# A trunk kernel's odd input stage: two pairs of column blocks in seven products, the third in plain chunks, and the mixing weights fetched in the gate stage

## The chip, the cores and the metric

One core of a Trainium2 chip runs the kernel. The metric is device time in microseconds (us). The kernel before took 1264.31 us, the median of 3 runs (1264.02 to 1265.02).

## The reference, cut to what matters

Two layers work on a sequence of 256 rows and 2048 features in fp32. Layer 0 (even) is a recurrence and an attention; layer 1 (odd) is a gated unit with position mixing. After each layer a gate stage adds a projected per-layer input. The change touches the odd layer and the gate stage ahead of it:

```python
def odd_mixer(hn, w_in, ln_g, ln_b, w_s, b_s, w_out):
    u, v, g = jnp.split(hn @ w_in, 3, axis=-1)        # three times 2048 columns
    u = jax.nn.gelu(u)
    v = layer_norm(jax.nn.gelu(v), ln_g, ln_b)
    ...                                               # v in chunks of 128 positions, 16 groups of 128
    mixed = jnp.einsum('gts,bcsgd->bctgd', ws, vc) + b_s.T[:, :, None]
    y = u * mixed.reshape(bsz, t, SG_WIDTH) * jax.nn.silu(g)
    return y @ w_out

h = h + per_layer_embedding(h, p[layer], pe_w[layer], pe_gate_norm[layer], pe_w_gate[layer])
```

## The kernel before, in words

Every large product multiplies 256 rows by a 2048 x 512 block of a weight matrix. Rows and weights are each split into a high and a low fp32r part, and a product is the sum of three matmuls (high by high, high by low, low by high). Weights stream through the core in chunks of 128 x 1024 fp32 (512 KB): two k-tiles of 128 rows by 512 columns.

`program` (L955) writes the list `self.chunks` for the whole kernel and then walks it. For each chunk, `feed` (L159) keeps loads (`issue_load`, L140, on SyncE's queue) up to nine chunks ahead and splits (`issue_split`, L146) three chunks ahead: ScalarE copies the raw chunk to `hi` (L152), VectorE subtracts to get `lo` (L153). Then the chunk's matmuls are issued, and unless the chunk is marked `half`, `advance` (L119) moves every task on by one step. A task is a generator with the work on a finished block: scaling, gelu, transposing, storing. `until` (L130) makes a task wait for another's result. Tiles of 128 x 512 fp32 come from one pool of 52 buffers (`buf`, L87), PSUM has 8 banks (L88), raw chunks have 14 buffers (L85), split chunks 5 (L86).

Two kinds of work fill the list. A **plain** block (`unit`, L168, by `wunit`, L195) is eight chunks of twelve matmuls of 512 columns (lines L186 to L188, tile `pg`): two row tiles, two k-tiles, three products. A **pair** (`spair`, L203) computes two column blocks at once, 1024 columns, by a scheme of seven products in place of eight on the half-size parts of the row and weight matrices: 28 chunks of six matmuls (lines L226 to L228, into the banks `Z`, `V`, `U`). Three of the seven weight operands come straight from memory; the other four are made in place: once a chunk has been split, GpSimd issues a DMA that adds the next weight chunk to the raw tile (L157), and that sum is split later as the next chunk of the chain. The row operands are differences that `sums` (L288) makes from the transposed rows; they are split like the rows (`ssum`). What the banks hold is put together by small adds (L234 to L259) into SBUF tiles.

The odd input stage has 12 column blocks, four each for v, u and g. In the kernel before, blocks 0 and 1 of each of the three are a pair and blocks 2 and 3 are plain (L983 to L985): 84 pair chunks and 48 plain ones. `zip` (L273) lists them so that one plain chunk follows every two pair chunks, and so that the first product of the next pair stands before the last product of this one. The tasks are `ov_task` (L853: scale, gelu, statistics), `ou_task` (L906: scale, gelu), and `og_task` (L929: silu, product, transpose, split for the next stage), which waits for `mix_task` (L912), which waits for the normalised v and for u. When all four v blocks are there, `ln` (L867) normalises them in the order 2, 3, 0, 1: for each block it fetches gain and bias rows, spread over 128 partitions, on SyncE's queue (L885), then VectorE does two passes per row tile (L889, L890):

```python
        for c in (2, 3, 0, 1):
            g = self.t(name="lng")
            b = self.t(name="lnb")
            for x, src in ((g, "ln_g"), (b, "ln_b")):
                ap = self.a[src]
                nc.sync.dma_start(x, bass.AP(tensor=ap.tensor, offset=ap.offset + c * 512, ap=[[0, 128], [1, 512]]))
```

`odd_params` (L894), started with the third plain block, fetches the mixing weights on GpSimd's queue in four tiles and clears a corner of each after it has landed (L902). The stage behind is the odd output projection (`add_h_task` with layer 1), whose chunks are taken in the order 4, 5, 6, 7, 2, 3, 0, 1. Ahead of the odd stage stands the gate stage of layer 0 (`gate_layer`, L949; `gate_task`, L805): four blocks of one embedding chunk and eight plain ones. Each of its tasks stores the rows, transposes them and splits them for the odd stage (`to_acts`, L755).

Of the kernel before, what the change touches and what calls it, by code (L numbers as in the profile page):

```python
# [57 lines left out]

LOADS_AHEAD = 5
# [19 lines left out]
class Trunk:  # L79
# [121 lines left out]


    def spair(self, p, acts, sums, post):  # L203


# [13 lines left out]
        def mm(b, a, c):  # L219
            def f(hi, lo):  # L220
                new = first(b)
                for k in range(2):
                    j = 2 * c + k
                    wh, wl = hi[:, k * 512:(k + 1) * 512], lo[:, k * 512:(k + 1) * 512]
                    ah, al = a(j, 0), a(j, 1)
                    nc.tensor.matmul(st[b], ah, wh, start=new and k == 0, stop=False, skip_group_check=True)  # L226
                    nc.tensor.matmul(st[b], al, wh, start=False, stop=False, skip_group_check=True)  # L227
                    self.last_mm = nc.tensor.matmul(st[b], ah, wl, start=False, stop=(c == 3 and k == 1),  # L228
                                                    skip_group_check=True)
                if c == 3:  # L230
                    after[b].pop(0)()
            return f
# [31 lines left out]
        for b, w, chain, a in (("Z", 0, 0, x(0, 0)), ("V", 1, 0, z(1)), ("Z", 2, 1, x(1, 0)), ("U", 3, 0, z(2)),  # L264
                               ("V", 3, 2, z(3)), ("U", 1, 2, z(0)), ("U", 2, 0, x(1, 1))):
            for c in range(4):
                q = Chunk(blk(w, c), 1024, mm(b, a, c), half=c % 2 == 0)
# [20 lines left out]
    def sums(self, pt, g):  # L288

        nc = self.nc  # L290
        xe = self.t([128, T], name="xe")
        nc.scalar.activation(xe, pt[:, 0], AF.Copy, scale=g[:, 0:1])
        a11, a21 = xe[:, 0:128], xe[:, 128:256]
        a12, a22 = pt[:, 1, 0:128], pt[:, 1, 128:256]
        s = self.t([128, 4, 128], name="s")
        nc.vector.scalar_tensor_tensor(s[:, 1], a22, g[:, 1:2], a21, op0=OP.mult, op1=OP.subtract)
        nc.vector.tensor_tensor(s[:, 0], a11, a21, op=OP.subtract)
        nc.vector.scalar_tensor_tensor(s[:, 3], a12, g[:, 1:2], a11, op0=OP.mult, op1=OP.subtract)
# [450 lines left out]
    def squares(self, h, key, c, t):  # L749
        if c == 0 and t == 0:  # L750
            self.ss[key] = self.kept([128, 2, 4], "ss")
        j = self.t(name="junk")
        self.nc.scalar.activation(j, h, AF.Square, accum_out=self.ss[key][:, t, c:c + 1])

    def to_acts(self, hs, c, key, gain_col):  # L755

        for p in range(2):
# [5 lines left out]
            if key in self.summed:  # L763
                self.spawn(self.sums_task(key, j, self.sums(pt, g)))
        for t in range(2):
            self.squares(hs[t], key, c, t)
        if c == 3:
            self.rms(self.ss[key], key)
# [19 lines left out]

    def add_h_task(self, c, layer, ps):
        if layer == 1:  # L790
            self.h[c] = []
            for t in range(2):
                h = self.t(name="hr")
                nc = self.nc
                nc.sync.dma_start(h, self.hd[c, t])
                self.h[c].append(h)
# [4 lines left out]
        yield  # L801
        self.to_acts(hs, c, f"g{layer}", C_PG + 16 * layer)
        yield

    def gate_task(self, c, layer, ps):  # L805
# [3 lines left out]
        e = self.e.pop((layer, c))  # L809
        hs = self.h[c]  # L810
# [11 lines left out]
        if layer == 0:  # L822
            for t in range(2):
                self.hd[c, t] = self.dram.tile([128, 512], F32, name=self.name("hd"))
                nc.sync.dma_start(self.hd[c, t], hs[t])
            yield 2
            self.to_acts(hs, c, "o", C_NG + 16)
            del self.h[c]
# [37 lines left out]

    def ln(self):  # L867
# [26 lines left out]
    def odd_params(self):  # L894
        nc, a = self.nc, self.a
        self.bs = self.kept([128, 16], "bs")
# [32 lines left out]
    def og_task(self, c, ps):  # L929
# [10 lines left out]
        for p in range(2):  # L940
            o = p * T
            self.y[2 * c + p] = self.split(self.fm(ys[0][:, o:o + T], ys[1][:, o:o + T], "yt"), scale=0.25)
# [6 lines left out]
    def gate_layer(self, layer):  # L949
        for c in range(4):  # L950
            self.put(self.unit([self.a["pe_w"][layer, c]], lambda: self.pT[layer],
                               lambda ps, c=c: self.e.__setitem__((layer, c), ps), nk=2, bank=self.pa))
            self.put(self.wunit(lambda: self.hs[f"g{layer}"], self.post(self.gate_task, c, layer)))

    def program(self):  # L955
# [5 lines left out]
        self.st = None  # L961
        self.xs, self.ssum, self.summed, self.hd = {}, {}, {"o"}, {}
# [27 lines left out]
        self.put(plain[:4])  # L990
        self.zip(plain[4:], pairs)
        n = len(self.chunks)
        for c in range(4):
            wu(lambda: self.y, self.add_h_task, c, 1, order=[4, 5, 6, 7, 2, 3, 0, 1])
        self.chunks[n + 8].spawn.append(lambda: self.load_p(1))
        self.gate_layer(1)
# [71 lines left out]
def _layout(i):  # L1068
# [24 lines left out]
    parts += [tm(wo[2048:]), tm(wo[:2048]), tm(wg[0]), tm(ov[:, 1024:]), tm(ou[:, 1024:]), tm(og[:, 1024:]), tm(oo), tm(wg[1])]  # L1093

    seven = lambda w: w.reshape(4, 2, 2, 128, 2, 512).transpose(2, 4, 0, 3, 1, 5).reshape(4, 4, 128, 1024)
    w7 = np.stack([seven(w) for w in (ov[:, :1024], ou[:, :1024], og[:, :1024])])
# [41 lines left out]
```

## Time and profile before

| | |
|---|---|
| median of 3 runs | 1264.31 us |
| the profiled execution | 1264.85 us, its span 1263.1 us |
| TensorE busy | 1237.7 us (98%) |
| VectorE, ScalarE, GpSimd busy | 859.6, 724.3, 113.2 us |
| moved by DMA | 266.70 MB, 211 GB/s on average |

Engines are PE (TensorE's matmuls), PEld (its weight loads), DVE (VectorE), ACT (ScalarE), POOL (GpSimd) and SP (SyncE, which only issues DMAs here). Matmuls are pipelined: each row shows 0.39 us for one of 512 columns, but the next begins 0.23 us later, so their rate is read from starts, and only a gap between them is idle time. By the lines, the odd input stage runs from about 808 to 1045 us of the span.

### The profile page before, as it was taken

The page shows a single profiled execution, that of the slowest core. Times are in us where ns is not written, and L with a number is a line of the kernel's source. Part 1 is how long each engine was busy: PE and PEld are TensorE (multiplying, and loading weights), DVE is VectorE, ACT ScalarE, POOL GpSimd, SP SyncE. Part 2 cuts the span into 40 slices and gives each one's busy share as a digit, 9 for nine tenths or more (in the row PEclk, how much of TensorE's full clock was granted, in tenths as well). Part 3 has the DMA queues.
Part 4 walks back from the last instruction along what each step waited for, and adds up shares of the span by engine and source line. Part 5 has one row for each costly group of instructions (what it writes and reads, how often), then busy time and mean ns, then how long its engine had stood idle before and what let it go on. Part 6 is the DMA issues. An engine that isn't in the chain of part 4 may idle for free.

```text
span 1263.1 us, 16229 instructions
## 1 busy us (share of the span) xinstructions
PE 1237.7 (98%) x5828; PEld 1033.0 (82%) x5828; DVE 859.6 (68%) x1283; ACT 724.3 (57%) x999; POOL 113.2 (9%) x138
## 2 busy tenths in 40 slices
PE   7999999999999999999999999999988999999998
PEld 7878888888888888888888888887866888888886
DVE  6658566567577778764555577776879978655554
ACT  6554445554576877843454556676746666545442
POOL 0000303023000010000000000221211110000000
PEclk9999999999999999999999999999999999999999
DMA  9987645555556465576655566899999998666620
GB/s 344 293 238 261 198 159 186 163 168 184 173 177 194 158 199 189 165 268 202 197 178 193 187 212 203 204 277 251 308 251 258 309 245 286 219 213 202 207 92 33
DMA packets 79920, 266.70 MB, mean 211 GB/s; under 512 B 8880, under 2 KB 11584, under 8 KB 79840
## 3 DMA queue, kind: packets, MB, share of 16 engines
q1 hardware_dynamic: 68976, 231.47, 54.2%
q0 software_dynamic: 8800, 31.06, 11.8%
q10 hardware_dynamic: 2064, 3.14, 1.9%
q8 instruction: 45, 0.74, 0.2%
q14 instruction: 35, 0.29, 0.1%
HBM read 258.31 MB, written 7.33 MB: 210 GB/s over the span
## 4 chain that ended last, share of the span: by engine, by line
PE 88%; DMA 4%; issue 3%; DVE 3%; POOL 1%; ACT 1%; SPq 0%; DVEq 0%; POOLq 0%; ACTq 0%
PE pg L186 25%; PE pg L187 25%; PE pg L188 25%; DMA lnb<-in_ln_b 2%; DVE lo L153 2%; DMA raw<-in_w 1%; PE ht L329 1%; PE U L226 1%; PE U L228 1%; PE U L227 1%; DMA lng<-in_ln_g 1%; PE pa L188 1%; PE pa L187 1%; PE pa L186 1%; POOL raw L157 1%
## 5 line engine op out<-in xcount | busy, mean ns | idle before, releaser
L153 DVE TENSOR_TENSOR lo<-raw,hi 128x1024 fp32r<-128x1024 f32 (+1 forms) x468 | 563.0, 1213 | 318.4 <-ACT hi L152 308.7
L152 ACT ACTIVATE hi<-raw 128x1024 fp32r<-128x1024 f32 (+1 forms) x468 | 486.2, 1046 | 454.2 <-PE pg L188 333.2
L186 PE MATMUL pg<-hi,xh 128*128 128x512 f32 (+1 forms) x1504 | 588.2, 391 | 6.8 <-ACT xh L312 6.3
L187 PE MATMUL pg<-lo,xh 128*128 128x512 f32 (+1 forms) x1504 | 582.4, 387 | 5.5 <-DVE lo L153 5.4
L188 PE MATMUL pg<-hi,xl 128*128 128x512 f32 (+1 forms) x1504 | 581.4, 387 | 0.0
L187 PEld LDWEIGHTS pg<-lo,xh 128*128 128x128 f32 x1504 | 283.4, 188 | 61.8 <-DVE lo L153 9.0
L186 PEld LDWEIGHTS pg<-hi,xh 128*128 128x128 f32 x1504 | 283.3, 188 | 61.5 <-ACT xh L312 6.3
L188 PEld LDWEIGHTS pg<-hi,xl 128*128 128x128 f32 x1504 | 283.0, 188 | 55.3
L157 POOL DMA_DIRECT2D raw<-in_w x48 | 41.5, 885 | 259.4 <-DVE lo L153 126.9
L228 PE MATMUL U<-lo,xh 128*128 128x512 f32 x72 | 28.1, 391 | 0.5 <-DVE lo L153 0.5
L226 PE MATMUL U<-hi,xh 128*128 128x512 f32 x72 | 28.2, 392 | 0.0
L227 PE MATMUL U<-hi,xl 128*128 128x512 f32 x72 | 28.0, 389 | 0.0
L689 POOL TENSOR_TENSOR tt<-tt,tg 128x512 f32<-128x512 f32 x8 | 10.3, 1293 | 172.9 <-ACT tt L687 172.9
L312 ACT ACTIVATE xh<-ht,cols 128x256 fp32r<-128x256 f32 x48 | 21.0, 468 | 8.4 <-DVE xl L313 8.1
L228 PE MATMUL Z<-lo,xh 128*128 128x512 f32 x48 | 19.3, 401 | 4.9 <-DVE lo L153 4.9
L313 DVE SCALAR_TENSOR_TENSOR xl<-ht,cols,xh 128x256 fp32r<-128x256 f32 x48 | 21.7, 479 | 3.4 <-ACT xh L312 2.9
L713 DVE SCALAR_TENSOR_TENSOR xc<-xat,cols,xc 128x255 f32<-128x255 f32 (+2 forms) x48 | 22.2, 477 | 0.5
L340 POOL TENSOR_TENSOR rg<-s,mhalf 128x2 f32<-128x2 f32 x2 | 1.4, 718 | 229.2 <-DVE s L338 229.2
L817 ACT ACTIVATE z<-pg,rg 128x512 f32<-128x512 f32 (+1 forms) x18 | 11.2, 641 | 17.4 <-PE pg L188 17.4
L562 POOL TENSOR_TENSOR rq<-rq,mhalf 128x8 f32<-128x8 f32 x4 | 7.6, 1906 | 148.2 <-DVE rq L561 148.2
L228 PE MATMUL V<-lo,xh 128*128 128x512 f32 x48 | 18.8, 392 | 1.6 <-DVE lo L153 1.6
L226 PE MATMUL Z<-hi,xh 128*128 128x512 f32 x48 | 19.0, 396 | 0.0
(256 smaller groups left out, 1029.5 us busy)
## 6 DMA issues: line engine op xcount, KB each, us to landing
raw<-in_w SPq DMA_DIRECT2D x388, 512.0 KB, 4.4
raw<-in_w POOLq DMA_DIRECT2D x48, 512.0 KB, 9.8
raw<-in_idx_w SPq DMA_DIRECT2D x24, 368.0 KB, 7.4
raw<-in_pe_w SPq DMA_DIRECT2D x8, 512.0 KB, 3.7
bias_d<-bt ACTq DMA_DIRECT2D x1, 3064.0 KB, 35.1
x<-in_xT SPq DMA_DIRECT2D x8, 256.0 KB, 6.8
xn<-in_x SPq DMA_DIRECT2D x8, 256.0 KB, 7.0
bias<-bias_d POOLq DMA_DIRECT2D x8, 256.0 KB, 3.8
```

What stands on the lines that cost most here:

```text
L152: nc.scalar.activation(hi[:, :c.cols], raw, AF.Copy)
L153: self.last_lo = nc.vector.tensor_tensor(lo[:, :c.cols], raw, hi[:, :c.cols].bitcast(F32), op=OP.subtract)
L157: nc.gpsimd.dma_start(c.raw, c.next.ap, accum_op=OP.add)
L186: self.nc.tensor.matmul(ps, xh, wh, start=(c == order[0] and k == 0), stop=False)
L187: self.nc.tensor.matmul(ps, xh, wl, start=False, stop=False)
L188: self.last_mm = self.nc.tensor.matmul(ps, xl, wh, start=False, stop=(c == order[-1] and k == 1))
L226: nc.tensor.matmul(st[b], ah, wh, start=new and k == 0, stop=False, skip_group_check=True)
L227: nc.tensor.matmul(st[b], al, wh, start=False, stop=False, skip_group_check=True)
L228: self.last_mm = nc.tensor.matmul(st[b], ah, wl, start=False, stop=(c == 3 and k == 1), skip_group_check=True)
L312: nc.scalar.activation(hi[:, s], src[:, s], AF.Copy, scale=g)
L313: nc.vector.scalar_tensor_tensor(lo[:, s], src[:, s], g, hi[:, s].bitcast(F32), op0=OP.mult, op1=OP.subtract)
L713: nc.vector.scalar_tensor_tensor(xc[:, s, k:], xa[:, s, :T - k], col(C_CW + (3 - k) * 16 + f), xc[:, s, k:], op0=OP.mult, op1=OP.add)
```

## The change

`PAIRED` and `O_PAIRS` are new constants. With the values given, only the odd input stage's v and u blocks 0 and 1 are done as pairs; all four g blocks are plain. The other paths that the diff adds (pairs in the gate stages and in the output projection, parking rows in memory there) are not taken. `zip` no longer puts a plain chunk after every second pair chunk: it spreads `free` plain chunks evenly over the pair chunks, keeps three for the place before the last product, and leaves `tail` (10) to the end. The gain and bias rows of blocks 2 and 3 are fetched in `odd_params`, those of blocks 0 and 1 at the first two steps of `ln`, all on GpSimd's queue. `odd_params`, with the mixing weights, starts with the nineteenth chunk of the gate stage of layer 0, its third block. The output projection takes its chunks in the order 0 to 7.

```diff
+PAIRED = ('o',)
+O_PAIRS = 2
...
-    def zip(self, cs, pairs):
+    def zip(self, cs, pairs, tail=0, extra=((), ())):
...
-            ss += p[:24] if i == 0 else p[4:24]
-            ss += (pairs[i + 1][:4] if i + 1 < len(pairs) else [None] * 3) + p[24:]
-        out = []
-        for i, q in enumerate(ss):
-            if q is not None:
-                out.append(q)
-            if (q is None or i % 2) and cs:
-                out.append(cs.pop(0))
+            last = i + 1 == len(pairs)
+            ss += p[0 if i == 0 else 4:20]
+            ss += [None, *extra[0], *p[20:24], *extra[1]] if last and extra[0] else p[20:24]
+            ss += ([None] * (2 if extra[1] else 3) if last else pairs[i + 1][:4]) + p[24:]
+        n = len(ss) - ss.count(None)
+        free = len(cs) - tail - ss.count(None)
+        out, due = [], 0
+        for q in ss:
+            if q is None:
+                out.append(cs.pop(0))
+                continue
+            out.append(q)
+            due += free
+            if due >= n:
+                due -= n
+                out.append(cs.pop(0))
         self.chunks += out + cs
...
+    def load_ln(self, c):
+        self.lnp[c] = []
+        for src in ("ln_g", "ln_b"):
+            x = self.t(name=src)
+            ap = self.a[src]
+            self.nc.gpsimd.dma_start(x, bass.AP(tensor=ap.tensor, offset=ap.offset + c * 512, ap=[[0, 128], [1, 512]]))
+            self.lnp[c].append(x)
...
-        for c in (2, 3, 0, 1):
-            g = self.t(name="lng")
-            b = self.t(name="lnb")
-            for x, src in ((g, "ln_g"), (b, "ln_b")):
-                ap = self.a[src]
-                nc.sync.dma_start(x, bass.AP(tensor=ap.tensor, offset=ap.offset + c * 512, ap=[[0, 128], [1, 512]]))
+        for i, c in enumerate((2, 3, 0, 1)):
+            g, b = self.lnp.pop(c)
+            if i < 2:
+                self.load_ln(i)
             yield
...
     def odd_params(self):
         nc, a = self.nc, self.a
+        for c in (2, 3):
+            self.load_ln(c)
+            yield 3
...
-        self.gate_layer(0)
+        mark = len(self.chunks)
+        self.gate_layer(0, index.get("g0"))
+        by2, by4 = self.come("g0")
+        self.chunks[mark + 18].spawn.append(self.odd_params)
...
-        plain = [self.wunit(hs, self.post(task, c)) for task in (self.ov_task, self.ou_task, self.og_task) for c in (2, 3)]
-        pairs = [self.spair(i, hs, so, [self.post(task, 0), self.post(task, 1)])
-                 for i, task in enumerate((self.ov_task, self.ou_task, self.og_task))]
+        tasks = (self.ov_task, self.ou_task, self.og_task)
+        plain = [self.wunit(hs, self.post(task, c), order=by2)
+                 for i, task in enumerate(tasks) for c in range(2 if i < O_PAIRS else 0, 4)]
+        pairs = [self.spair(len(PAIRED) + i - 1 if i else index["o"], hs, so, [self.post(task, 0), self.post(task, 1)],
+                            order=by4) for i, task in enumerate(tasks[:O_PAIRS])]
         for c in range(4):
             plain[2][0].spawn.append(lambda c=c: self.mix_task(c))
-        plain[2][0].spawn.append(self.odd_params)
...
-        self.zip(plain[4:], pairs)
+        self.zip(plain[4:], pairs, tail=3 if O_PAIRS == 3 else 10)
         n = len(self.chunks)
-        for c in range(4):
-            wu(lambda: self.y, self.add_h_task, c, 1, order=[4, 5, 6, 7, 2, 3, 0, 1])
+        self.stage("y", "o" if O_PAIRS == 3 else "", index.get("y"), lambda: self.y, self.add_h_task, 1)
```

## Rows read from the trace of the kernel before

**Rows 1.** The page, part 1: busy time and share of the span of PE, PEld, DVE, ACT and POOL, with counts of instructions.

```profile
PE 1237.7 (98%) x5828; PEld 1033.0 (82%) x5828; DVE 859.6 (68%) x1283; ACT 724.3 (57%) x999; POOL 113.2 (9%) x138
```

**Rows 2.** Busy time by stretches of the span. Columns: the stretch, its length, then busy time (and instructions) of PE, PEld, DVE, ACT and POOL, the granted clock of TensorE, the busy share of the 16 DMA engines, and GB/s.

```profile
10.00:806.00 796.00, 793.56 (x3834) 667.14 (x3833) 532.33 (x887) 459.94 (x676) 61.31 (x68) 1.00 0.63 203
860.00:960.00 100.00, 88.31 (x378) 69.69 (x377) 79.81 (x101) 63.05 (x75) 19.38 (x26) 0.98 0.98 275
808.50:1045.00 236.50, 224.81 (x1008) 183.59 (x1007) 194.34 (x245) 155.18 (x184) 46.73 (x58) 0.99 0.99 269
1045.00:1250.00 205.00, 205.00 (x934) 170.28 (x933) 124.57 (x135) 101.03 (x126) 2.29 (x3) 1.00 0.56 184
1250.00:1263.10 13.10, 8.13 (x36) 6.38 (x35) 2.81 (x8) 1.68 (x4) 0.00 (x0) 0.98 0.12 40
```

**Rows 3.** Waits of PE from 800 to 1100 us: who waited for whom, us in total, times, and the longest.

```profile
PE Z L228 <- DVE lo L153: 4.9, 1, 4.9
PE pg L187 <- DVE lo L153: 4.5, 5, 1.7
PE V L228 <- DVE lo L153: 1.6, 1, 1.6
PE U L228 <- DVE lo L153: 0.5, 1, 0.5
```

**Rows 4.** The timeline of all engines from 903 to 966 us, cut to the first fetch of a gain row and what waited for it. Columns: start and duration in us, engine, line, operation, tiles, shapes, count, and in brackets the idle time of the engine before it with what ended it. SPq is SyncE issuing a DMA.

```profile
905.91 0.39 PE L186 MATMUL pg<-hi,xh 128*128 128x512 f32 x1
...
906.59 0.39 PE L186 MATMUL pg<-hi,xh 128*128 128x512 f32 x1
...
908.07 0.47 SPq L885 DMA_DIRECT2D lng<-in_ln_g  x1
...
915.66 0.39 PE L227 MATMUL Z<-hi,xl 128*128 128x512 f32 x1
918.98 0.75 DVE L889 SCALAR_TENSOR_TENSOR v<-v,s,lng 128x512 f32<-128x512 f32 x1 [6.81 <-DMA lng<-in_ln_g]
919.64 2.35 DVE L153 TENSOR_TENSOR lo<-raw,hi 128x1024 fp32r<-128x1024 f32 x2
...
920.92 0.61 PE L228 MATMUL Z<-lo,xh 128*128 128x512 f32 x1 [4.87 <-DVE lo L153]
...
921.33 0.63 PE L226 MATMUL Z<-hi,xh 128*128 128x512 f32 x1
...
924.31 0.51 PE L187 MATMUL pg<-lo,xh 128*128 128x512 f32 x1
```

**Rows 5.** The timelines of VectorE (two rows) and of ScalarE (one row), in the same columns, at the third block of the norm (block 0).

```profile
946.41 0.75 DVE L889 SCALAR_TENSOR_TENSOR c<-c,s,lng 128x512 f32<-128x512 f32 x1 [4.12 <-DMA lng<-in_ln_g]
...
949.74 0.75 DVE L890 SCALAR_TENSOR_TENSOR c<-c,s,lnb 128x512 f32<-128x512 f32 x1 [1.44 <-DMA lnb<-in_ln_b]
...
946.89 1.06 ACT L152 ACTIVATE hi<-raw 128x1024 fp32r<-128x1024 f32 x1 [6.52 <-DMA raw<-in_w]
```

**Rows 6.** Groups of instructions over the whole span, by line (the last, of VectorE, from 860 to 960 us): count, busy us, mean ns of one, idle time before them and what ended it.

```profile
L153 DVE TENSOR_TENSOR lo<-raw,hi 128x1024 fp32r<-128x1024 f32 (+1 forms) x468 | 563.0, 1213 | 318.4 <-ACT hi L152 308.7
L152 ACT ACTIVATE hi<-raw 128x1024 fp32r<-128x1024 f32 (+1 forms) x468 | 486.2, 1046 | 454.2 <-PE pg L188 333.2
...
L849 ACT ACTIVATE ge<-ge 128x512 f32<-128x512 f32 x16 | 9.8, 620 | 1.3 <-DVE ge L845 1.3
...
L845 DVE SCALAR_TENSOR_TENSOR ge<-ge,c 128x512 f32<-128x512 f32 x3 | 2.1, 694 | 0.5 <-ACT ge L844 0.5
```

**Rows 7.** DMA from 808.5 to 1045 us: two queues (q0 is GpSimd's) with MB and their share of 16 engines' time, and issues by line with KB each and the median us from issue to landing.

```profile
q0 software_dynamic: 6944, 25.17, 54.4%
q1 hardware_dynamic: 11104, 38.34, 44.2%
...
raw<-in_w SPq DMA_DIRECT2D x69, 512.0 KB, 7.9
raw<-in_w POOLq DMA_DIRECT2D x46, 512.0 KB, 10.1
ws<-in_wsT POOLq DMA_DIRECT2D x4, 256.0 KB, 6.8
lng<-in_ln_g SPq DMA_DIRECT2D x4, 256.0 KB, 8.5
lnb<-in_ln_b SPq DMA_DIRECT2D x4, 256.0 KB, 8.8
```

**Rows 8.** DMA from 706 to 806 us, the gate stage of layer 0, in the same columns.

```profile
q1 hardware_dynamic: 5996, 19.71, 59.7%
...
raw<-in_w SPq DMA_DIRECT2D x33, 512.0 KB, 4.3
```

**Rows 9.** Waits of POOL from 800 to 1100 us, in the columns of the third group.

```profile
POOL raw L157 <- DVE lo L153: 126.9, 35, 17.0
...
POOL ws L902 <- DMA ws<-in_wsT: 13.0, 4, 6.8
```

**Rows 10.** Waits of SyncE's queue from 850 to 960 us, in the same columns.

```profile
SPq L885 <- DVE p L889: 4.8, 1, 4.8
...
SPq L885 <- DVE u L850: 3.9, 2, 3.1
```

More of the change, by code (lines that the diff above doesn't have):

```diff
@@ L200, in put, with spair @@
             self.chunks += x
-    def spair(self, p, acts, sums, post):
+    def spair(self, p, acts, sums, post, order=(0, 1, 2, 3)):
         nc = self.nc
@@ L227, in f @@
                     nc.tensor.matmul(st[b], al, wh, start=False, stop=False, skip_group_check=True)
-                    self.last_mm = nc.tensor.matmul(st[b], ah, wl, start=False, stop=(c == 3 and k == 1),
+                    self.last_mm = nc.tensor.matmul(st[b], ah, wl, start=False, stop=(c == order[3] and k == 1),
                                                     skip_group_check=True)
-                if c == 3:
+                if c == order[3]:
                     after[b].pop(0)()
@@ L265, in spair @@
                                ("V", 3, 2, z(3)), ("U", 1, 2, z(0)), ("U", 2, 0, x(1, 1))):
-            for c in range(4):
-                q = Chunk(blk(w, c), 1024, mm(b, a, c), half=c % 2 == 0)
+            for i, c in enumerate(order):
+                q = Chunk(blk(w, c), 1024, mm(b, a, c), half=i % 2 == 0)
                 q.follows(chains.get((chain, c)))
@@ L749, in squares @@
     def squares(self, h, key, c, t):
-        if c == 0 and t == 0:
+        if key not in self.ss:
             self.ss[key] = self.kept([128, 2, 4], "ss")
+            self.nss[key] = 0
         j = self.t(name="junk")
@@ L787, in add_x_task, with park, fetch @@
         self.h[c] = xs
+    def park(self, c):
+        hs = self.h.pop(c)
+        for t in range(2):
+            self.hd[c, t] = self.dram.tile([128, 512], F32, name=self.name("hd"))
+            self.nc.sync.dma_start(self.hd[c, t], hs[t])
+    def fetch(self, c):
+        self.h[c] = []
+        for t in range(2):
+            h = self.t(name="hr")
+            self.nc.sync.dma_start(h, self.hd[c, t])
+            self.h[c].append(h)
     def add_h_task(self, c, layer, ps):
         if layer == 1:
[L791 to L796, printed above, removed]
+            self.fetch(c)
             yield
@@ L801, in add_h_task @@
         yield
+        if layer == 1 and "g1" in PAIRED:
+            self.park(c)
         self.to_acts(hs, c, f"g{layer}", C_PG + 16 * layer)
@@ L809, in gate_task @@
         e = self.e.pop((layer, c))
+        if layer == 1 and "g1" in PAIRED:
+            self.fetch(c)
+            yield
         hs = self.h[c]
@@ L822, in gate_task @@
         if layer == 0:
-            for t in range(2):
-                self.hd[c, t] = self.dram.tile([128, 512], F32, name=self.name("hd"))
-                nc.sync.dma_start(self.hd[c, t], hs[t])
+            self.park(c)
             yield 2
             self.to_acts(hs, c, "o", C_NG + 16)
-            del self.h[c]
         yield
@@ L941, in og_task @@
             o = p * T
-            self.y[2 * c + p] = self.split(self.fm(ys[0][:, o:o + T], ys[1][:, o:o + T], "yt"), scale=0.25)
+            yt = self.fm(ys[0][:, o:o + T], ys[1][:, o:o + T], "yt")
+            self.y[2 * c + p] = self.split(yt, scale=0.25)
+            if "y" in PAIRED:
+                self.spawn(self.sums_task("y", 2 * c + p, self.sums(yt, (0.25, 0.25))))
         yield
@@ L947, in post, with come, stage, gate_layer @@
         return lambda ps: self.spawn(task(*args, ps), delay)
[L949 to L953, printed above, removed]
+    def come(self, key):
+        return ([4, 5, 6, 7, 2, 3, 0, 1], (2, 3, 1, 0)) if key in PAIRED else (list(range(8)), (0, 1, 2, 3))
+    def stage(self, key, prev, p, acts, task, *args, before=None, lead=5, tail=0):
+        pre = (lambda c: before(c)) if before else (lambda c: [])
+        order, by4 = self.come(prev)
+        if key not in PAIRED:
+            for c in range(4):
+                self.put(pre(c), self.wunit(acts, self.post(task, c, *args), order=order))
+            return
+        plain = sum((pre(c) + self.wunit(acts, self.post(task, c, *args), order=order) for c in (2, 3)), [])
+        pair = self.spair(p, acts, lambda: self.ssum[key], [self.post(task, c, *args) for c in (0, 1)], order=by4)
+        self.put(plain[:lead])
+        self.zip(plain[lead:], [pair], tail, (pre(1), pre(0)))
+    def gate_layer(self, layer, p, **kw):
+        e = lambda c: self.unit([self.a["pe_w"][layer, c]], lambda: self.pT[layer],
+                                lambda ps: self.e.__setitem__((layer, c), ps), nk=2, bank=self.pa)
+        self.stage(f"g{layer}", "y" if layer else "", p, lambda: self.hs[f"g{layer}"], self.gate_task, layer, before=e, **kw)
     def program(self):
@@ L960, in program @@
         self.h, self.hs, self.pT, self.e, self.ov, self.u, self.y = {}, {}, {}, {}, {}, {}, {}
[L961 to L962 removed]
+        self.nss = {}
+        self.st, self.lnp = None, {}
+        self.xs, self.ssum, self.hd = {}, {}, {}
         xs = lambda: self.xs
```

30 lines of the change are left out of this document (17 added, 13 removed).

## The prediction

> **What bounds the kernel now.** I read the busy times first: TensorE is busy 98% of the span [rows 1], so a change pays only through TensorE's own work or through the 25 us in which it idles. The table of stretches says where those are [rows 2]. From 10 to 806 us it idles 796.00 - 793.56 = 2.4 us, from 1045 to 1250 not at all, at the end some 5 us, which the change doesn't reach. The odd input stage, 808.5 to 1045, has 236.50 - 224.81 = 11.7 us, all of it between 860 and 960 (100.00 - 88.31). The DMA engines are busy 0.98 to 0.99 of that stage, against 0.56 to 0.63 outside it.
>
> The list of waits names what ends each of TensorE's: VectorE's `lo` split, eight times, 11.5 us in all, 4.9 us the longest [rows 3]. But VectorE isn't late for its own sake: the timeline around the longest wait shows it idle for 6.81 us before L889, until a gain row lands whose fetch was issued at 908.07 [rows 4]. VectorE works in the order it is given, so the splits behind L889 stood still, and TensorE, with about 2 us of split chunks in hand (6.81 against 4.87), ran dry. At block 0 the same comes again: 4.12 and 1.44 us for gain and bias, and beside it ScalarE waits 6.52 us for a raw chunk [rows 5]. So the stage is TensorE's, with holes from late transfers.
>
> **The change part by part.** The sum is made against the profiled execution, 1264.85 us, 0.54 us above the median.
>
> *More matmuls.* A pair is 28 x 6 = 168 matmuls of 512 columns, two plain blocks 2 x 8 x 12 = 192: 24 more. Three matmuls start within 906.59 - 905.91 = 0.68 us [rows 4], so one is 0.227 us and 24 are **+5.4 us**. Nothing hides them. (The Trainium skill, "TensorE: Matmul & The Clock Gate", section "Wait — 56ns, not 53.3ns?", gives 215.7 ns between starts of 512 columns at the full clock; by it an estimate of 24 x 0.2157 = 5.2 us. This trace has 227 ns, and I go by that.)
>
> *Less DMA.* GpSimd's queue took 0.544 x 236.5 = 128.7 us of the 16 engines for 25.17 MB, 5.1 us a MB; SyncE's took 104.5 us for 38.34 MB, 2.7 us a MB [rows 7]. A chunk of 0.524 MB is thus 2.7 us when added, 1.4 us when loaded plainly. The third pair takes away 16 added and 12 loaded chunks and 16 plain ones come: -42.9 + 5.7 us. The mixing weights (four of 0.26 MB, at GpSimd's price) and two blocks' gain and bias go to another stage: some -8 us. From 233 us it falls to 188 in a stage of about 230 us: a share of 0.82 in place of 0.99.
>
> *Room in the chains.* A chunk of a pair lasts 6 x 0.227 = 1.36 us, a plain one 2.72. Where one product directly follows another of its chain, its chunk must be added, landed and split within four pair chunks and the plain ones between: before, 4 x 1.36 + 2 x 2.72 = 10.9 us, against 10.1 us to land [rows 7], so anything late shows. After, 60 - 10 - 3 = 47 plain chunks go between 56 pair chunks: 4 x 1.36 + 3.36 x 2.72 = 14.6 us, 4.5 us to spare. That should end the small `lo` waits.
>
> *The gain and bias rows.* Blocks 2 and 3 are fetched a stage earlier and cost nothing at the norm: the wait of 6.81 us goes. Blocks 0 and 1 are still fetched inside the stage, at the norm's first two steps, on GpSimd's queue. In the order of the program block 0's first use is about six steps behind its fetch, with some 2.5 us a step; against 8.5 us to land [rows 7] that is enough if the instructions keep that distance. In the trace they don't: the use stood ready before the row (4.12 us early at block 0, [rows 5]). Its cost is between 0 and what the first fetch costs now, 6.6 us (4.9 idle, 1.6 clock, 0.2 refill, below). With block 2's and 3's eight passes ahead of it I take 1.5 us, nearer nothing.
>
> *Mixing weights in the gate stage.* The four clears waited 13.0 us on GpSimd for their landing, with additions queued behind them [rows 9]; that goes. In the gate stage the eight fetches of 256 KB meet a DMA share of 0.60 and loads that land in 4.3 us [rows 8], issued up to nine chunks (24 us) ahead: nothing at the forecast, and if the loads slowed to the stage's 7.9 us [rows 7] they would still be in time. GpSimd has nothing else to do there.
>
> *Buffers.* Counted by the program, the odd stage holds 32 split row and difference tiles; now with 4 mixing and 4 gain and bias tiles from its start. When `ln` starts there are 8 tiles of v, 4 of u (a plain u block is done earlier relative to the pairs), 2 of the second pair, 2 fetched rows and a gelu tile: 57 for 52 buffers. Before, the same count peaked at 53, and even so SyncE's fetches of gain rows waited 4.8 and 3.9 us for the tiles of L889 and L850 to be freed [rows 10]. Something will wait longer here; what it delays (a scaling of u, a fetch) has PSUM banks and steps to spare. Between 0 and 12 us (priced as a rival below), I take 1.0.
>
> *Order at the end.* After the last product ten plain chunks of g remain. u's block 0 needs five steps for gelu, then three to mix, one for silu, two to the transposes: y's first tiles are issued one chunk (2.7 us) ahead of the output projection's first. Transposes, a ScalarE pass of 0.62 us and a VectorE pass of 0.69 us [rows 6] fit in. Between 0 and 2 us: 0.5. The chunk order 0 to 7 only follows that. The splits fall by 12, 12 x 1.21 us of VectorE and 12 x 1.05 us of ScalarE [rows 6]: off the path, it helps the last 0.5 us that I leave for small waits.
>
> **The sum.** What can go: idle 11.7 us; TensorE's clock fell to its lower level after the longest wait, 920.92 to 924.31 for eight matmuls, 3.39 us in place of 1.82, so 1.6 us; and the first start after a wait is late by more than the idle time, 920.92 - 915.66 - 0.23 = 5.03 against 4.87, 0.16 us for each of eight, 1.3 us [rows 3, 4]. Together 14.6. What stays: 1.5 + 1.0 + 0.5 + 0.5 = 3.5. 1264.85 + 5.4 - 14.6 + 3.5 = 1259.2, and 0.5 off for the median: **1258.6 us**. What a measurement can tell from no change is about 0.2%, 2.5 us: faster is below 1261.8, slower above 1266.8.
>
> **The rivals.**
> *Every hole closes.* The DMA share of 0.82 speaks for it; the buffer count against it. 1264.85 + 5.4 - 14.6 - 0.5 = 1255.1, and some refill that I could not see in these rows might go too: 1253 to 1256.
> *The stop moves to block 0.* The fetch of block 0's gain takes the place of block 2's: issued late for want of a buffer and landing in 8.5 us, used at once. Then 6.6 us stay in place of 1.5: 1258.6 + 5.1 = 1263.7, no change that can be told. For it: the 4.12 + 1.44 us already seen there [rows 5]. Against: eight passes of blocks 3 and 2 now come in between without a stop. (The Trainium skill speaks for this rival: "DMA: Bandwidth & Descriptors", section "Issuing engines are not separate DMA queues", says that all queues run on the same 16 engines, so GpSimd's queue by itself makes no fetch faster. The trace agrees in so far as the mixing weights took 6.8 us on that queue beside 8.5 and 8.8 on SyncE's [rows 7].)
> *GpSimd's queue is held.* A fetch of block 0 or 1 waits there for a buffer, and the additions behind it wait too. GpSimd has waited 17.0 us for VectorE at one instruction [rows 9]. Less 4.5 us to spare in the chain and 2 us in hand, 10.5 us idle, with the clock 12.1, in place of 1.0: 1258.6 + 11.1 = 1269.7, slower. It decides from a hold of about 14 us. Against: what frees the tiles no longer waits for a transfer.
> *VectorE was the cause after all.* If the eight waits come from its load (79.81 us of 100 in that stretch [rows 2]) and only move, the matmuls are added and nothing is won: 1264.3 + 5.4 = 1269.7. Against: its 6.81 us of idleness.
>
> **How the numbers follow.** Forecast 0.50 (1256 to 1261), every hole closes 0.17, the stop moves 0.18, the queue is held 0.08, VectorE 0.07. The range 1253.5 to 1266 holds the first three but for a little. Faster: 0.50 + 0.17 + 0.04 of the third = 0.71. Same: the other 0.14 and 0.02 of the held queue = 0.16. Slower: 0.13.
>
> **What would show it.** TensorE's matmuls from 5828 to 5852; the DMA share of the odd stage near 0.8; no wait before L889 at blocks 2 and 3; TensorE's idle time in the stage 2 to 4 us and the clock at its upper level throughout; the stage about 6 us shorter. It would be wrong if `lo` waits of several us stand at block 0 or 1, if additions stand behind fetches on GpSimd's queue, or if TensorE waits at the first chunk of the output projection.

## The result, and the profile after

The changed kernel takes 1254.15 us (median of 4 runs, 1254.05 to 1254.36) against 1264.16 us for the kernel before (4 runs, 1262.84 to 1265.02): a ratio of 0.9916 (0.9904 to 0.9927), 10 us faster. The forecast was 1258.6 us. What came is the first rival, "every hole closes", that had been given 1253 to 1256 us and a chance of 0.17; it lies 0.65 us above the lower end of the stated range.

The page of the changed kernel, parts 1 and 4 (busy times as in [rows 1]; then the chain of work that ended last, by engine):

```profile
PE 1238.0 (99%) x5852; PEld 1037.1 (83%) x5852; DVE 842.7 (67%) x1266; ACT 713.4 (57%) x985; POOL 102.9 (8%) x130
...
PE 98%; DMA 1%; DVE 0%; ACT 0%; SPq 0%; POOL 0%; issue 0%; DVEq 0%; POOLq 0%
```

There are 24 matmuls more, as many as were counted, and yet the span is 1252.5 us in place of 1263.1. Busy time by stretches of the changed kernel, in the columns of [rows 2]:

```profile
860.00:960.00 100.00, 100.00 (x451) 83.07 (x450) 85.15 (x103) 69.19 (x82) 16.43 (x20) 1.00 0.96 272
...
808.50:1050.00 241.50, 241.50 (x1108) 201.26 (x1107) 196.69 (x249) 157.06 (x184) 32.62 (x39) 1.00 0.89 253
1050.00:1240.00 190.00, 190.00 (x864) 157.85 (x863) 106.82 (x114) 88.35 (x111) 1.71 (x2) 1.00 0.52 168
1240.00:1252.50 12.50, 7.28 (x33) 5.68 (x31) 2.81 (x8) 1.68 (x4) 0.00 (x0) 0.98 0.13 43
```

Where 11.7 us were idle before [rows 2] there are none: TensorE is busy in every one of 241.50 us, and its clock stays at the upper level (granted 1.00). The section on the profile before lets the stage end at 1045 us, which is too early: by its last matmuls it runs from 808.0 to 1067.6 us before and from 808.3 to 1057.6 after, so that it is some 10 us shorter (the forecast had about 6). The windows to 1045 and to 1050 us lie inside it, and no hole of before stands between 1045 and its end [rows 2]. The waits of TensorE over the whole span, in the columns of [rows 3]:

```profile
PE pg L188 <- ACT xh L322: 6.7, 1, 6.7
PE ikt L445 <- DVE ikd L439: 1.1, 1, 1.1
PE pg L189 <- DVE lo L155: 1.0, 2, 0.5
PE pg L188 <- ACT hi L154: 0.5, 1, 0.5
```

None of these lies in the odd stage: all end before 46 us. The eight waits for `lo` [rows 3] are gone, not moved. DMA from 808.5 to 1050 us of the changed kernel, in the columns of [rows 7]:

```profile
q1 hardware_dynamic: 12074, 43.96, 51.3%
q0 software_dynamic: 4720, 17.04, 37.4%
...
raw<-in_w SPq DMA_DIRECT2D x84, 512.0 KB, 5.8
raw<-in_w POOLq DMA_DIRECT2D x30, 512.0 KB, 8.1
ln_g<-in_ln_g POOLq DMA_DIRECT2D x2, 256.0 KB, 5.8
ln_b<-in_ln_b POOLq DMA_DIRECT2D x2, 256.0 KB, 7.5
```

GpSimd's queue carries 17 MB in place of 25, an added chunk lands in 8.1 us in place of 10.1, and a product of a chain now follows another after 14.6 us (worked out in the prediction), not 10.9. ScalarE's waits for raw chunks [rows 5] are gone from the stage: before they were 23.1 us in 10 waits, every one for an added chunk. Who waited for the additions (L157) of the kernel before, and how long these took to land; then the landing of those of the changed kernel (L159), for which ScalarE never waited:

```profile
  ACT hi L152: 23.1, 10
...
DMA to landing us min/median/max: 5.4/9.8/13.7
```

```profile
DMA to landing us min/median/max: 5.4/7.9/10.5
```

VectorE still stops once for a gain row. Its timeline there:

```profile
941.04 5.76 DVE L155 TENSOR_TENSOR lo<-raw,hi 128x1024 fp32r<-128x1024 f32 x5
946.72 0.74 DVE L917 SCALAR_TENSOR_TENSOR c<-c,s,ln_g 128x512 f32<-128x512 f32 x1
...
949.96 2.35 DVE L155 TENSOR_TENSOR lo<-raw,hi 128x1024 fp32r<-128x1024 f32 x2
...
956.80 1.41 DVE L917 SCALAR_TENSOR_TENSOR c<-c,s,ln_g 128x512 f32<-128x512 f32 x2 [3.83 <-DMA ln_g<-in_ln_g]
...
959.17 2.35 DVE L155 TENSOR_TENSOR lo<-raw,hi 128x1024 fp32r<-128x1024 f32 x2
```

The stop of 3.83 us is at block 1; block 0, at 946.72, has its row in time. TensorE doesn't feel it: eight splits were made from 941.04 to 952.31 us, and they last beyond the next ones, which begin at 959.17. Before, a stop of 4.12 us at the norm's third block went with idle time, and raw chunks were late there as well [rows 5].

### The profile page after: what moved, and what is told of

It is laid out like the page before. It is cut to its first block, busy times and chain, and to the rows that moved or that the text cites. A ratio compares the mean times of both kernels' runs of the same rounds, so it can differ in the third digit from the quotient of the medians.

```text
span 1252.5 us, 16196 instructions
## 1 busy us (share of the span) xinstructions
PE 1238.0 (99%) x5852; PEld 1037.1 (83%) x5852; DVE 842.7 (67%) x1266; ACT 713.4 (57%) x985; POOL 102.9 (8%) x130
## 4 chain that ended last, share of the span: by engine, by line
PE 98%; DMA 1%; DVE 0%; ACT 0%; SPq 0%; POOL 0%; issue 0%; DVEq 0%; POOLq 0%
PE pg L188 28%; PE pg L190 28%; PE pg L189 28%; PE U L230 1%; PE U L228 1%; PE U L229 1%; PE ht L339 1%; PE Z L228 1%; PE pa L190 1%; PE pa L188 1%; PE V L230 1%; PE V L228 1%; PE Z L230 1%; PE V L229 1%; PE pa L189 1%; PE Z L229 1%
## 5 line engine op out<-in xcount | busy, mean ns | idle before, releaser
L155 DVE TENSOR_TENSOR lo<-raw,hi 128x1024 fp32r<-128x1024 f32 (+1 forms) x456 | 548.2, 1211 | 334.1 <-ACT hi L154 325.8
L188 PE MATMUL pg<-hi,xh 128*128 128x512 f32 (+1 forms) x1568 | 612.4, 391 | 7.2 <-ACT xh L322 6.7
L189 PE MATMUL pg<-lo,xh 128*128 128x512 f32 (+1 forms) x1568 | 605.9, 386 | 1.0 <-DVE lo L155 1.0
L190 PE MATMUL pg<-hi,xl 128*128 128x512 f32 (+1 forms) x1568 | 605.8, 386 | 0.0
L188 PEld LDWEIGHTS pg<-hi,xh 128*128 128x128 f32 x1568 | 295.0, 188 | 64.0 <-ACT xh L322 6.7
L190 PEld LDWEIGHTS pg<-hi,xl 128*128 128x128 f32 x1568 | 294.7, 188 | 58.0
L189 PEld LDWEIGHTS pg<-lo,xh 128*128 128x128 f32 x1568 | 295.0, 188 | 57.0 <-DVE lo L155 1.5
L159 POOL DMA_DIRECT2D raw<-in_w x32 | 27.8, 868 | 147.7 <-DVE lo L155 107.9
L699 POOL TENSOR_TENSOR tt<-tt,tg 128x512 f32<-128x512 f32 x8 | 10.4, 1295 | 172.9 <-ACT tt L697 172.9
L843 DVE SCALAR_TENSOR_TENSOR z<-z,pa 128x512 f32<-128x512 f32 (+1 forms) x18 | 11.0, 622 | 11.5 <-ACT z L842 11.5
L598 POOL TENSOR_TENSOR bm<-bias,mb 128x256 f32<-128x256 f32 x16 | 15.7, 982 | 27.9 <-DMA bias<-bias_d 25.3
```

Source lines behind the costliest of these rows:

```text
L155: self.last_lo = nc.vector.tensor_tensor(lo[:, :c.cols], raw, hi[:, :c.cols].bitcast(F32), op=OP.subtract)
L159: nc.gpsimd.dma_start(c.raw, c.next.ap, accum_op=OP.add)
L188: self.nc.tensor.matmul(ps, xh, wh, start=(c == order[0] and k == 0), stop=False)
L189: self.nc.tensor.matmul(ps, xh, wl, start=False, stop=False)
L190: self.last_mm = self.nc.tensor.matmul(ps, xl, wh, start=False, stop=(c == order[-1] and k == 1))
```

## The experiments

Two theories for the holes stood against each other: "rows" (the gain and bias rows that come late to the norm) and "room" (the third pair's added chunks). In the code cuts, "..." stands for lines left out. All ratios are to the kernel before on the same chip.

**The third pair again, two ways.** e1_three_pairs:

```diff
-O_PAIRS = 2
+O_PAIRS = 3
```

> The changed kernel with all three pairs again (g's blocks 0 and 1 in seven products), rows and mixing weights still fetched early, plain chunks spread evenly. Theory 'rows' (the late gain and bias rows made the holes, and they go with the early fetch): 24 matmuls fewer and no holes, 1254.2 - 5.4 = 1249. Theory 'room' (the third pair's added chunks crowd the DMA engines and the chains, and only its absence closes the holes): the holes come back in part, some 8 to 10 us of them, 1257 to 1260, with the DMA share of the odd stage at 0.98.

1262.27 us, 0.9979 (0.9970 to 0.9988), slower than either theory said; the holes are back (TensorE busy 92.97 us of 100 from 860 to 960). e4_before_moved comes from the other side, the kernel before with the fetches moved:

```diff
-        for c in (2, 3, 0, 1):
-            g = self.t(name="lng")
-            b = self.t(name="lnb")
...
+        for i, c in enumerate((2, 3, 0, 1)):
+            g, b = self.lnp.pop(c)
+            if i < 2:
+                self.load_ln(i)
             yield
...
+        for c in (2, 3):
+            self.load_ln(c)
+            yield 3
         self.bs = self.kept([128, 16], "bs")
...
+        self.chunks[mark + 18].spawn.append(self.odd_params)
...
-        plain[2][0].spawn.append(self.odd_params)
```

> The kernel before with nothing but the fetches moved (rows of blocks 2 and 3 and the mixing weights in the gate stage, rows of blocks 0 and 1 at the norm's first two steps on GpSimd's queue); three pairs, a plain chunk after every second pair chunk. Theory 'rows': the holes behind the norm go, 1264.2 - 10 to 14 = 1250 to 1254. Theory 'room': the stop before block 2 goes, the late added chunks stay or move, 1257 to 1262.

1257.69 us, 0.9942 (0.9927 to 0.9957), at the low end of what "room" said. Moving the fetches alone wins some 7 us, and holes are left. In both kernels ScalarE waits for raw chunks; e4_before_moved, its stretch from 860 to 960 us and the waits of ScalarE from 808 to 1050:

```profile
860.00:960.00 100.00, 96.14 (x418) 77.16 (x417) 90.09 (x112) 68.32 (x81) 20.45 (x24) 0.98 0.99 275
```

```profile
ACT hi L152 <- PE pg L188: 22.8, 15, 2.8
ACT hi L152 <- DMA raw<-in_w: 22.5, 12, 5.1
```

e1_three_pairs has 30.0 us of that in 10 waits, 10.7 the longest. It spreads 38 plain chunks over 84 pair chunks: 4 x 1.36 + 1.81 x 2.72 = 10.4 us between chained products, 0.5 us less than e4_before_moved. The output projection takes its chunks in the same order in both (4, 5, 6, 7, 2, 3, 0, 1: with three pairs the new code keeps it), so what differs is how the plain chunks are set among the pair chunks.

**The rows late, with two pairs.** e2_rows_late:

```diff
-            self.nc.gpsimd.dma_start(x, bass.AP(...))
+            self.nc.sync.dma_start(x, bass.AP(...))
...
         for i, c in enumerate((2, 3, 0, 1)):
+            self.load_ln(c)
             g, b = self.lnp.pop(c)
-            if i < 2:
-                self.load_ln(i)
...
-        for c in (2, 3):
-            self.load_ln(c)
-            yield 3
```

> The changed kernel, with the gain and bias rows of all four blocks fetched inside the norm on SyncE's queue as before; two pairs, mixing weights early. Theory 'rows': VectorE stops before L889's counterpart for block 2 again, TensorE idles some 5 us there and its clock falls once: 1260 to 1264. Theory 'room': VectorE may stop, but TensorE has enough split chunks in hand: 1254 to 1256.

1260.90 us, 0.9969 (0.9956 to 0.9981), as "rows" said, but not at the block that it named. Waits of VectorE in e2_rows_late from 808 to 1050 us, and of TensorE from 800 to 1100:

```profile
DVE c L917 <- DMA ln_b<-in_ln_b: 4.3, 1, 4.3
DVE c L916 <- DMA ln_g<-in_ln_g: 3.1, 1, 3.1
DVE v L917 <- DMA ln_b<-in_ln_b: 2.1, 1, 2.1
...
DVE v L916 <- DMA ln_g<-in_ln_g: 0.9, 1, 0.9
```

```profile
PE U L230 <- DVE lo L155: 3.2, 1, 3.2
PE pg L189 <- DVE lo L155: 1.1, 2, 0.9
```

Tile `v` is a plain block, 2 or 3; `c` here is block 0, at 963 and 969 us. The stops at blocks 2 and 3 are short, and TensorE is busy all the time from 860 to 960 us. Those at block 0 reach TensorE, whose granted clock is 0.98 from 960 to 1050 us. So both theories hold in part, and the four kernels make a table:

| ratio to before | rows fetched in the norm | rows and weights early |
|---|---|---|
| three pairs, packed as before | 1 | 0.9942 (e4_before_moved) |
| two pairs, plain chunks spread | 0.9969 (e2_rows_late) | 0.9916 (the change) |

The rows are worth 0.0058 with three pairs and 0.0053 with two, 7 us either way; the upper figure has the mixing weights in it, which the lower left kernel has early already. (The next run says that these don't matter with two pairs; with three it was not tried.) The lower row drops the third pair and spreads the plain chunks, and it takes the output projection's chunks in the order 0 to 7, where TensorE has no wait in either order. Together that is worth 0.0031 and 0.0026, 3 to 4 us: 5.4 us of matmuls paid, 9 us of holes closed.

**The mixing weights.** e3_mix_late:

```diff
             yield 3
+
+    def odd_mix(self):
+        nc, a = self.nc, self.a
         self.bs = self.kept([128, 16], "bs")
...
+        plain[2][0].spawn.append(self.odd_mix)
```

> The changed kernel with the mixing weights fetched and cleared in the odd stage as before; gain and bias rows early. If the clears that wait on GpSimd's queue held the additions back enough to make holes: 1257 to 1260. If they were covered: 1254 to 1255, with the wait of some 13 us for the weights' landing back on GpSimd and no idle time of TensorE.

1254.18 us, 0.9918 (0.9904 to 0.9933): with two pairs that part of the change does nothing. GpSimd waits 5.9 us for the weights, not some 13, and TensorE has no idle time. The waits of GpSimd from 800 to 1060 us, and the stage:

```profile
POOL ws L936 <- DMA ws<-in_wsT: 5.9, 3, 3.8
```

```profile
808.50:1050.00 241.50, 241.50 (x1107) 201.36 (x1106) 196.77 (x249) 156.96 (x184) 36.02 (x47) 1.00 0.89 258
```

**The density of added chunks.** e5_half_density:

```diff
-            due += free
+            due += n // 2
             if due >= n:
```

> The changed kernel with the pairs packed as before: one plain chunk after every second pair chunk (28 in place of 47 between the pair chunks, 29 in place of 10 left for the end). Two pairs, the same bytes, rows and weights early; but 10.9 us in place of 14.6 from one product of a chain to the next, and the added chunks crowded into a shorter stretch. If room in the chains closed the holes that are left in e4_before_moved: they come back, 2 to 6 us of idle time, 1257 to 1261, ScalarE waiting for raw chunks. If it is only that the third pair's bytes are gone: 1254 to 1255.

1261.72 us, 0.9979 (0.9969 to 0.9988), 0.7 us above the range for "room". With the same bytes and the same rows, only packed as before, the holes are back. e5_half_density, its stretch from 860 to 960 us and ScalarE's waits from 808 to 1050:

```profile
860.00:960.00 100.00, 95.94 (x411) 76.89 (x410) 90.05 (x112) 68.74 (x82) 18.69 (x22) 0.97 0.99 277
```

```profile
ACT hi L154 <- PE pg L190: 51.2, 33, 2.6
ACT hi L154 <- DMA raw<-in_w: 17.0, 8, 5.1
```

So what dropping the third pair wins hangs on spreading the other two over the plain chunks that take its place. Against e4_before_moved, which has the same fetches and the same packing with three pairs, this kernel is 0.0037 slower, 4.7 us, not far from the 5.4 us of its 24 matmuls more: leaving out the third pair pays nothing by itself.

**The price of an addition.** e7_moved_plain, against e4_before_moved:

```diff
-            nc.gpsimd.dma_start(c.raw, c.next.ap, accum_op=OP.add)
+            nc.gpsimd.dma_start(c.raw, c.next.ap)
```

> The kernel e4_before_moved (three pairs, fetches moved) with the second and later weight chunks of a chain copied over the raw tile in place of added to it, on the same queue: the sums of weights are left out. Same packets and waits, but no reading back of the tile. If the price of an addition on the DMA engines (5.1 us a MB beside 2.7) makes the small holes: the share of the odd stage falls to some 0.8, they close, 1249 to 1252. If the wait for the split and the landing is what counts: within 1.5 us of 1257.7.

1248.44 us, 0.9874 (0.9859 to 0.9888), 0.6 us below the range of the first case: with copies in place of additions the same three pairs run without a hole. e7_moved_plain, the odd stage and its GpSimd transfers:

```profile
808.50:1045.00 236.50, 236.50 (x1086) 197.18 (x1085) 207.53 (x258) 167.08 (x195) 31.24 (x55) 1.00 0.82 281
```

```profile
q0 software_dynamic: 7024, 25.43, 31.9%
...
raw<-in_w POOLq DMA_DIRECT2D x46, 512.0 KB, 4.6
```

It also shows that VectorE has the time for three pairs: 207.53 us of 236.50.

**DMA load without additions.** e8_extra_copies was to add plain transfers to the stage:

```diff
             self.nc.sync.dma_start(c.raw[:, :c.cols], c.ap)
+        if 0 <= j - self.odd0 < 96 and j % 6 == 0:
+            x = self.dram.tile([128, 1024], F32, name=self.name("xtra"))
+            self.nc.sync.dma_start(x, c.ap)
...
+        self.odd0 = len(self.chunks)
```

> The changed kernel with sixteen more transfers of 512 KB (weights copied to unused memory) on SyncE's queue over the odd stage: the chains keep their 14.6 us of room, the DMA engines get back roughly the bytes of the third pair. If the DMA load by itself makes holes: share near 0.98 and 1256 to 1260. If room in the chains shields TensorE: 1254 to 1255.

1279.59 us, 1.0118 (1.0102 to 1.0135), for a reason of no use here: nothing held the sixteen transfers back, the scheduler issued them all between 78 and 98 us, and TensorE's longest wait, for a split, is 16.5 us. e9_extra_in_stage ties them to loads of the stage:

```diff
-            self.nc.sync.dma_start(c.raw[:, :c.cols], c.ap)
+            ld = self.nc.sync.dma_start(c.raw[:, :c.cols], c.ap)
+            if j >= self.odd0 + 8 and self.extra < 12:
+                self.since += 1
+                if self.since % 4 == 0:
+                    self.extra += 1
+                    x = self.dram.tile([128, 1024], F32, name=self.name("xtra"))
+                    with self.tc.issue_after(ld.ins):
+                        self.nc.sync.dma_start(x, c.ap)
...
+        self.odd0, self.extra, self.since = len(self.chunks), 0, 0
```

> The changed kernel with twelve more transfers of 512 KB, each tied behind a chunk's load in the odd stage (in e8_extra_copies the scheduler put such transfers near the start of the kernel, so that run says nothing on the stage). Chains keep their 14.6 us of room. If the DMA load by itself makes holes: share of the odd stage near 0.95, ScalarE waiting for raw chunks, 1256 to 1262. If room shields TensorE: 1254 to 1255.

1253.97 us, 0.9914 (0.9899 to 0.9928), no slower than the change. e9_extra_in_stage, its stretch from 860 to 960 us and its added chunks from 808.5 to 1045:

```profile
860.00:960.00 100.00, 100.00 (x451) 83.10 (x450) 84.28 (x102) 69.03 (x82) 16.42 (x20) 1.00 1.00 304
```

```profile
raw<-in_w POOLq DMA_DIRECT2D x30, 512.0 KB, 8.3
```

The DMA engines are full (1.00, against 0.98 in [rows 2]) and TensorE has no hole. A share near 1 was not what made the holes before.

**More room only where products are chained.** e10_uneven:

```diff
-O_PAIRS = 2
+O_PAIRS = 3
...
+        for p in pairs:
+            for i, q in enumerate(p):
+                q.share = 1.8 if i // 4 in (0, 1, 4, 5) else 0.3
+        n = sum(q.share for q in ss if q is not None)
...
-            due += free
+            due += free * q.share
```

> e1_three_pairs (three pairs, fetches early) with the same plain chunks, but set where a product directly follows another of its chain: 0.70 of a plain chunk behind each pair chunk of the first, second, fifth and sixth product, 0.12 behind the others; four pair chunks and 2.8 plain ones, 13.0 us from one product of a chain to the next in place of 10.4. If room between chained products is what was lacking: the waits for raw chunks mostly go, 1250 to 1255, faster than e4_before_moved (1257.7) and perhaps than the changed kernel. If the DMA engines or VectorE limit three pairs (stretches with hardly any plain chunk ask a split of every 1.4 us): 1258 to 1264.

1266.75 us, 1.0018 (1.0010 to 1.0027), the slowest of the three-pair kernels, against the "room" expectation and above the other range too. ScalarE's waits for raw chunks there: 23.9 us in 5 waits, 10.5 the longest, though 13.0 us lie between directly chained products. DMA of e10_uneven from 920 to 948 us, around the longest wait:

```profile
q0 software_dynamic: 1181, 4.20, 70.8%
...
raw<-in_w POOLq DMA_DIRECT2D x5, 512.0 KB, 17.2
```

So it isn't the interval alone. Added chunks land later here: 17.2 us, against 12.8 in e4_before_moved in the same 28 us and 8.5 in the changed kernel. It isn't the bytes of that stretch either, since e4_before_moved added 4.58 MB in it and e10_uneven 4.20 MB.

What orders the landings is how many additions are under way. Counted from the issue and the landing of each in the traces, for those issued from 808 to 1050 us:

| median us to landing, with so many others under way at the issue | 0 | 1 | 2 | 3 | 4 |
|---|---|---|---|---|---|
| before | 7.6 | 8.8 | 10.3 | 11.7 | |
| e10_uneven | 7.9 | 8.7 | 8.7 | 12.5 | 16.9 |
| the change | 5.9 | 7.5 | 9.4 | | |
| e7_moved_plain (copies) | 4.5 | 4.3 | 5.6 | | |

In the changed kernel there are never more than two. In each of eight kernels counted (before, the change, e1, e2, e4, e5, e9, e10) additions land in the order of their issue, and one with two or more ahead of it lands 3.6 to 3.9 us (median) behind the one before it; a copy of e7_moved_plain 1.4 us. So additions that are issued faster than one in some 3.7 us pile up behind each other. The packing of before asks for four in 10.9 us where products are chained, one in 2.7 us; the change asks for one in 3.65 us (14.6 / 4). Over the stage the median from one issue to the next is 2.9 us before and 4.1 us after. What holds an addition to that rate is not shown; in e9_extra_in_stage, with the DMA engines full, it is 3.7 us as well.

**Pairs in stages with more room.** v_o_y and v_o_g1 use the code's own switch:

```diff
-PAIRED = ('o',)
+PAIRED = ('o', 'y')
```

> The changed kernel with a pair in the output projection as well (blocks 0 and 1 in seven products, the code's own path): 24 matmuls fewer there, where the DMA share was 0.52 and TensorE never idle. If nothing gets in the way: 1254.2 - 5.4 = 1249. If its sums of rows, made at the end of the odd stage, or its chains come late: 1252 to 1258.

1259.56 us, 0.9960 (0.9945 to 0.9975), above both ranges. In v_o_y TensorE's waits from 1040 us on:

```profile
PE ht L339 <- DVE hr L820: 6.1, 3, 3.9
PE U L228 <- ACT hi L154: 0.6, 1, 0.6
```

v_o_y_early takes the first of these away:

```diff
+    def early(self, c):
+        self.fetch(c)
+        yield
...
         if layer == 1:
-            self.fetch(c)
             yield
...
+        for i, c in enumerate((2, 3, 1, 0)):
+            self.chunks[n + 6 + 8 * i].spawn.append(lambda c=c: self.early(c))
```

> v_o_y (pairs in the odd input stage and in the output projection) with the stored rows fetched before a block's product is done, not after: in v_o_y VectorE waited 8.9 us for them and TensorE 6.1 us for the transposes behind. If that fetch was all that kept the 24 matmuls' gain: 1248 to 1251, faster than both kernels. If the added chunks behind it are late too: 1252 to 1258.

1260.56 us, 0.9966 (0.9954 to 0.9979), above both ranges again. The wait went (0.7 us), and another came; TensorE's waits in v_o_y_early from 800 us on, and its DMA from 1085 to 1125:

```profile
PE U L228 <- ACT hi L154: 6.0, 2, 4.7
PE ht L339 <- DVE hr L823: 0.7, 1, 0.7
```

```profile
q0 software_dynamic: 1503, 5.44, 66.7%
...
raw<-in_w POOLq DMA_DIRECT2D x9, 512.0 KB, 12.9
```

Added chunks land in 12.9 us there too. And v_o_g1, `PAIRED = ('o', 'g1')`:

> The changed kernel with a pair in the last gate stage (the code's own path): 24 matmuls fewer where the DMA share was 0.52 and nothing waits. 1249 if the end is no longer than before; its last blocks come out of the pair together and rows are fetched back from memory for them, which may lengthen the 5 us tail: 1250 to 1256.

1257.61 us, 0.9943 (0.9928 to 0.9958), above both ranges. The 24 matmuls are saved, but in the profiled execution (1259.51 us, the slowest of four) 7.3 us of waits for splits stand around the last pair (`U` after `hi` 3.1, after `lo` 2.5, `pg` 1.7), with the granted clock at 0.96 from 1200 us on. No version tried that still computes everything is faster than the changed kernel beyond the noise.

## Why the prediction was right, and where it was off

The direction was right, and so were the two causes that it named, the late rows and the chains. The size was not: 10.0 us in place of 5.7, within the range because that was made wide enough for the first rival.

**More matmuls, +5.4 us**: 5852, and three start within 0.68 us as before (955.45 - 954.77 in the changed kernel). Right.

**The rows**: right, and shown by e2_rows_late and e4_before_moved. The forecast didn't put a figure on this part alone; it is 7 us of the 10. In e2_rows_late the loss comes at block 0, so that the earlier fetch of block 0 is a part of the gain and not only that of blocks 2 and 3. The rival "the stop moves to block 0" counted 6.8 us beside 8.5 and 8.8 [rows 7] for itself; those rows say rather that a fetch on GpSimd's queue was no slower.

**Room in the chains and less DMA**: right in outcome, partly wrong in reason. The DMA share was forecast at 0.82 and came to 0.89 (both queues took a little more a MB, 5.3 and 2.8 us in place of 5.1 and 2.7); and e9_extra_in_stage shows that the share isn't what matters, e5_half_density beside e4_before_moved that fewer bytes alone close nothing. What matters is how late added chunks land against the next use, and that depends on how closely they are issued (e5_half_density, e10_uneven) and on what one costs (e7_moved_plain). The forecast took the landing time as fixed, at 10.1 us; it fell to 8.1, because fewer additions were under way at once.

**Mixing weights**: the forecast counted on additions held back by the clears, without a term of its own for it; e3_mix_late measures nothing for it, with two pairs.

**What stays, 3.5 us**: this is the term that was mis-sized; it is 0. The 1.5 us for the fetch inside the stage: VectorE did stop, 3.83 us, at block 1, but TensorE had split chunks in hand for more than 6 us (from 952.97, where VectorE stops, to 959.17), not the 2 us taken from the trace of before; there, raw chunks came late beside the stops [rows 5]. The 1.0 us for buffers: GpSimd did wait for one. Its timeline in the changed kernel:

```profile
940.83 0.61 POOL L894 DMA_DIRECT2D ln_g<-in_ln_g  x1 [7.72 <-DVE u L872]
941.43 0.56 POOL L894 DMA_DIRECT2D ln_b<-in_ln_b  x1
947.10 0.89 POOL L159 DMA_DIRECT2D raw<-in_w  x1 [5.11 <-DVE lo L155]
950.33 0.56 POOL L894 DMA_DIRECT2D ln_g<-in_ln_g  x1 [2.34 <-DVE p L917]
```

The fetch of block 0 waited 7.72 us until a gelu tile was freed, far from the 14 us that the rival needed, and the next addition behind it waited for its own split, not for the fetch. The 0.5 us at the output projection and the 0.5 us of small waits: none.

**What can go, 14.6 us**: the profiled execution fell from 1264.85 to 1254.36 us, 10.5; with 5.4 of matmuls, 15.9 closed. Most of the 1.3 us between 14.6 and this can be read in the trace of before. The forecast counted that the first start after a wait comes 0.16 us late; the second start comes late as well, 0.34 us behind the first in place of 0.23. TensorE at one of the waits:

```profile
934.43 0.39 PE L186 MATMUL pg<-hi,xh 128*128 128x512 f32 x1
935.34 0.50 PE L187 MATMUL pg<-lo,xh 128*128 128x512 f32 x1 [0.52 <-DVE lo L153]
935.68 0.39 PE L188 MATMUL pg<-hi,xl 128*128 128x512 f32 x1
```

At all the waits but the longest the second start is some 0.11 us late, 0.8 us together. The rest is not placed.

So of the 4.5 us between forecast and result 3.5 are the stays and about 1 these late starts. The rivals on the slow side fell with the profile: VectorE, though 85.15 us of 100 busy from 860 to 960 us, holds nothing up, and e7_moved_plain runs it harder still (95.49 us of the same 100) without a hole.

## What to carry to other kernels

Seven products in place of eight save matmuls but cost transfers that add in place, and such a transfer lands later the more of them are under way: set the rate at which they are asked for against the rate at which they land (here one in some 3.7 us), and keep plain work between them. Leaving a pair out without that spreading won nothing (e5_half_density). A small operand of an engine that works in the order it is given (here 2 KB a partition of gain and bias) is worth buffers held for a stage if its late landing stops work that others wait for. What a stop costs depends on the stock at hand when it comes, so a price read where the stock was short is an upper end elsewhere.

## What the runs showed of the hardware

An addition on the way in costs 1.7 times the DMA time of a copy and takes twice as long to land: on the same queue, with the same packets, e4_before_moved took 54.8% of 16 engines for 25.43 MB (5.1 us a MB) and 9.5 us to land, e7_moved_plain 31.9% (3.0 us a MB) and 4.6 us. (The Trainium skill, "DMA: Bandwidth & Descriptors", section "Anatomy of one DMA — SWDGE (gpsimd) path", has a fit of 2.0 us plus the bytes over 436 GB/s, by which 512 KB would be an estimate of 3.2 us. The copies of e7_moved_plain took 4.6 us in a busy stretch; the additions of e4_before_moved, 9.5 us, are further from it.) Additions on one queue land one behind the other, some 3.7 us apart where they pile up. And sixteen DMA engines at a busy share of 1.00 for 100 us cost TensorE nothing in e9_extra_in_stage.
